# One plain gate moved into the first stage of a transformer layer, and w_out's operands moved later

## The chip, the core and the metric

The kernel runs on one core of a Trainium2 chip. The metric is device time in microseconds (us) for one execution. TensorE (PE in the profile) does the matmuls, ScalarE (ACT) and VectorE (DVE) make the operands and empty the accumulators, GpSimd (POOL) helps in the attention stage, and SyncE (SP) issues every DMA in one queue, in order.

## The reference, cut to what matters

One layer on a sequence of 1024 tokens with 1024 channels, float32:

```python
h = x @ w_in                                   # 8 blocks of q/k/v columns, then 2 x 1024 gate columns
qa, ka, va, qb, kb, vb, ga, gb = split(h)
y_a = chunk_band_attention(qa, ka, va) @ w_proj_a      # 8 heads, softmax over a band, learned bias
y_b = stick_breaking_attention(qb, kb, vb) @ w_proj_b  # 8 heads, running products, strictly causal
mix = (sigmoid(ga + bias) * y_a + sigmoid(gb + bias) * y_b) @ w_out
x = layer_norm(ALPHA * x + mix)
x = layer_norm(ALPHA * x + (silu(x @ w_g) * (x @ w_u)) @ w_ffn_out)
```

The 2048 gate columns are 16 gates of 128 columns each. Gate `i` is the product of a 1024 x 128 granule of `w_in` with all of `x`, and its value is needed only when the two attention branches are merged.

## The kernel before, in words

**Precision.** Every operand is split into a high and a low part (`split`, lines 110 to 112: a cast on ACT, then a subtraction on DVE), and each product is three matmuls: high x high, high x low, low x high. A block of 128 rows by 512 columns is one matmul instruction.

**Two ways to make a product.** A *plain* product of a 1024 x 128 granule with `x` is 8 x 3 matmuls for each half of the tokens, 48 in all. A *pair* of granules can instead be made by a 2 x 2 block scheme with 7 products (steps `p1`, `p2`, `p6`, `p5`, `p7`, `p3`, `p4` in `pair_steps`, 12 matmuls each, 84 instead of 96), which needs sums of the blocks of `x` (`s13`, `s24`, made once on DVE) and sums of the blocks of the two granules (`prep_right`, `prep_last`, made per pair on DVE and ACT).

**Stages.** The order of time is:

1. The q/k pairs. The first one (`project_plain(0)`) is made plainly, 96 matmuls into four accumulators of the `tr` and `pv` banks, because `s13` and `s24` are not there yet; its function returns a closure `take` that empties the accumulators. Then `run_pairs(1, N_QK, 2, also)` makes pairs 1 to 7 by the 7 products, with steps `p1` and `p2` of pairs 1 and 2 ahead of all others, since these two need only the left granule and parts of `x`, no sums.
2. `v_stage`, the values of both branches.
3. `run_pairs(N_QK, ...)`: five gate pairs (work items 8 to 12), which make gates 0 to 9 and store them to DRAM (`g_dr`).
4. The attention stage: 8 heads of branch A, then 8 of branch B. Its PE work consists of scores (`sc_a`, `sc_b`), transposes of the weights (`tp_a`, `tp_b`) and products with the values (`pv_a`, `pv_b`). Between them stands *fill*: single matmuls from a generator, `fill_all`, which makes the six plain gates 10 to 15 (288 matmuls) and then the projection of branch A (192). `FILL` says how many fill matmuls a head of A and of B draws; 8 x (18 + 42) = 480 is the sum of both.
5. The projection of branch B, `w_out`, the first LayerNorm, the FFN and the second LayerNorm.

**w_out's operands.** `w_out` is also multiplied by the 7-product scheme. Its 28 operand tiles are made early and stored to DRAM (`wo_dr`) by `wo_right(part)`, 12 parts (four blocks of three parts: the first loads two raw tiles and makes two operands, the second makes three, the third two). The table `wo_at` says behind which step `(i, j)` of the pairs each part stands, `i` the work item and `j` the index of the step in the list `p1, p2, p6, p5, p7, p3, p4`.

**Buffers.** Tiles take turns in groups of slots of 4 KB per partition. The ones that matter here: `gt` (3 slots: raw granules, gate results), `op` (8: split granules), `kp` (4), `v` (2: raw `w_out` tiles, later the heads' values), and `qs`, `kh`, `kl` (2 each), which are dealt out in turn by `cycle(QK, ...)` to the pairs' results and to w_out's operands, and later by name to the heads' q and k. `xt` (16) holds the split `x`. Accumulators are eight banks: `mm` 2, `sc` 2, `tr` 3, `pv` 1.

**What sets the order.** The program is traced in the order of the code; a scheduler then orders each engine's instructions by that priority and by a cost model, so an instruction whose inputs and slots are ready in the model can stand earlier than in the code. On the chip each engine takes its instructions strictly in the order so fixed, and an instruction that must wait holds up all behind it on its engine, SP's DMA issues too.

Lines that the change and the prediction touch: `FILL` (42), `split` (111, 112), `prep_left`, `prep_right`, `prep_last` (133 to 168), the products of the pairs (178), `project_plain` (118 to 121, 324, 325), `wo_right` (494 to 515), `load_gate` and `load_w` (524 to 526), `gate` (542, 545), `soft_block` and `stick_block` (632 to 670), the transposes and their split (696, 111, 112), the products with the values (710, 711, 720).

Of the kernel before, what the change touches and what calls it, by code (L numbers as in the profile page):

```python
# [38 lines left out]
PACKS = ((((4,), (5, 7), (3,), (2, 0), (6, 1)), ((7,), (6, 4), (5,))),  # L39
         (((4,), (5,), (6,), (7,), (3,), (2, 0), (1,)), ((7,), (6, 4), (5,))))  # L40

FILL = (18.0, 42.0)

# [5 lines left out]
def hybrid_trunk_kernel(ctx: ExitStack, tc, x, xt, w_in, w_v, b_gate, rel_bias, w_proj,  # L51
# [14 lines left out]
    def slot(tag, name, dtype=F32):  # L66
        return pool.tile([P, 1024], dtype, tag=tag, name=name, bufs=SLOTS[tag])
# [3 lines left out]
    def cycle(tags, name, dtype=F32):  # L71

        turn_of[tags] = turn_of.get(tags, -1) + 1
        return slot(tags[turn_of[tags] % len(tags)], name, dtype)

    QKV = ("qs", "kh", "kl", "v")
    QK = QKV[:3]

    def bank(tag, name):
        return ps.tile([P, HW], F32, tag=tag, name=name, bufs=BANKS[tag])  # L80
# [6 lines left out]
    dma = nc.sync.dma_start  # L87
# [22 lines left out]
    def split(dst_h, dst_l, src):  # L110
        nc.scalar.copy(dst_h, src)  # L111
        nc.vector.tensor_tensor(dst_l, src, dst_h.bitcast(F32), ALU.subtract)  # L112

    def mm3(acc, pairs):
        n = len(pairs)
        i = 0
        for lh, ll, rh, rl in pairs:
            mm(acc, lh, rh, start=(i == 0), stop=False)
            mm(acc, lh, rl, start=False, stop=False)
            i += 1  # L120
            mm(acc, ll, rh, start=False, stop=(i == n))
# [13 lines left out]
    def prep_left(W, nm, src, tag="op"):  # L135
        L = W["L"] = slot("gt", f"wL{nm}")
        load_then(L, src)
        W["hl"] = split_w(L, f"wl{nm}", tag)

    def split_w(raw, nm, tag):  # L140
        h = slot(tag, f"{nm}h", F32R)
        l = slot(tag, f"{nm}l", F32R)
        split(h, l, raw)
        return h, l
# [15 lines left out]
    def prep_last(W, nm, tag):  # L160

        c = slot(tag, f"wc{nm}", F32R)
        split(c[:, LO], c[:, HI], W["R"][:, HI])
        W["c"] = c
# [69 lines left out]
    N_GATE = 5  # L234
# [3 lines left out]
    def left(i):  # L238
        prep_left(Wa[i], f"p{i}", w_in[work[i][2]])

    def right(i):
        prep_right(Wa[i], f"p{i}", w_in[work[i][3]], "op")
        prep_last(Wa[i], f"p{i}", "kp")

    sops = {}
    s_tags = iter(["bw"] * 9 + ["pt"] * 4 + ["yt"] * 3)
    for kt in range(4):
# [21 lines left out]
        dma(xraw[k][:, HI], xt[k * P:(k + 1) * P, HI])  # L269
    for k in order_k:  # L270
        split(xh[k][:, HI], xl[k][:, HI], xraw[k][:, HI])
    for kt in range(4):
        a, b = xraw[kt], xraw[kt + 4]
        s13 = slot("kp", f"s13_{kt}")
        s24 = slot("kp", f"s24_{kt}")
        nc.vector.tensor_tensor(s13[:, LO], a[:, HI], b[:, HI], ALU.add)
        nc.vector.tensor_tensor(s24[:, LO], s13[:, LO], a[:, LO], ALU.subtract)
        nc.vector.tensor_tensor(s24[:, HI], b[:, LO], s24[:, LO], ALU.subtract)
        nc.vector.tensor_tensor(s13[:, HI], a[:, LO], a[:, HI], ALU.subtract)
        for src, nm in ((s24, "s24"), (s13, "s13")):  # L280
            split(*sops[nm, kt], src)
# [19 lines left out]
    def store_hl(d, hi, lo):  # L301
        for h in range(2):
            rows = slice(h * DH, (h + 1) * DH)
            dma(d[h * P:h * P + DH], hi[rows].bitcast(F32))
            dma(d[h * P + DH:(h + 1) * P], lo[rows])

    def project_plain(i):

        W, pair = Wa[i], work[i][1]
        accs = {}  # L310
        for half in (LO, HI):
            for side, key in enumerate(("hl", "hr")):
                tag = "pv" if side and half == HI else "tr"
                acc = accs[side, half.start] = bank(tag, f"plain{side}_{half.start}")
                wh, wl = W[key]
                mm3(acc, [(wh[:, k * P:(k + 1) * P], wl[:, k * P:(k + 1) * P],
                           xh[k][:, half], xl[k][:, half]) for k in (0, 4, 1, 5, 2, 6, 3, 7)])
        def take():
            for side, (scale, d) in enumerate(((-0.125, q_dr), (1.0, k_dr))):
                h = cycle(QK, f"hi{side}_{i}", F32R)  # L320
                t = cycle(QK, f"lo{side}_{i}")
                for half in (LO, HI):
                    acc = accs[side, half.start]
                    nc.scalar.activation(h[:, half], acc, AF.Copy, scale=scale)
                    nc.vector.scalar_tensor_tensor(t[:, half], acc, scale,
                                                   h[:, half].bitcast(F32),
                                                   ALU.mult, ALU.subtract)
                store_hl(d[pair], h, t)
        return take
# [36 lines left out]
    def run_pairs(lo, hi, first, also):  # L366

        steps = {i: project(i) for i in range(lo, hi)}
        for i in range(lo, lo + first):
            steps[i][0]()  # L370
            steps[i][1]()
        for i in range(lo, hi):
            for j, p in enumerate(steps[i][2:] if i < lo + first else steps[i]):
                p()
                if j == 0 and i + 1 < hi:
                    right(i + 1)
                if j == 1 and lo + 2 <= i + 2 < hi and i + 2 >= lo + first:
                    left(i + 2)
                also(i, j)
# [138 lines left out]
    def load_w(srcs, name, raw, hl, lo_eng):  # L518
        r = raw(f"wr_{name}")
        hi = hl(f"wh_{name}", F32R)  # L520
        lo = hl(f"wl_{name}", F32R)
        srcs = srcs if isinstance(srcs, list) else [(slice(0, 1024), srcs)]
        for cs, src in srcs:
            dma(r[:, cs], src)
        nc.scalar.copy(hi, r)
        lo_eng.tensor_tensor(lo, r, hi.bitcast(F32), ALU.subtract)
        return hi, lo

    def of(tag):
        return lambda name, dtype=F32: slot(tag, name, dtype)  # L530

    def load_gate(i, lo_eng):
        return load_w(w_in[24 + (i % 2) * 8 + i // 2], f"g{i}", of("op"), of("op"), lo_eng)

    def gate(i, w):
        gt = slot("gt", f"gate{i}")
        for hf, cs in enumerate((LO, HI)):
            acc = bank("mm", f"gps{i}_{hf}")
            for k in range(KT):
                ks = slice(k * P, (k + 1) * P)  # L540
                for j, (lw, rx) in enumerate(((w[0], xh), (w[0], xl), (w[1], xh))):
                    mm(acc, lw[:, ks], rx[k][:, cs], start=(k == j == 0),  # L542
                       stop=(k == KT - 1 and j == 2))
                    yield 1.0
            nc.scalar.copy(gt[:, cs], acc)
        dma(g_dr[i], gt)

    left(2)
    take = project_plain(0)
    right(1)  # L550
    take()
    wo_at = {(2, 4): 0, (3, 6): 1, (4, 6): 2, (5, 6): 3, (6, 2): 4, (6, 6): 5,
             (8, 6): 6, (9, 2): 7, (9, 6): 8, (10, 6): 9, (11, 2): 10, (11, 6): 11}

    def also(i, j):
        if (i, j) == (2, 2):
# [7 lines left out]
    run_pairs(1, N_QK, 2, also)  # L564
    v_stage()
    run_pairs(N_QK, len(work), 0, also)
    first_gate = 2 * N_GATE
    first_w = load_gate(first_gate, nc.vector)


# [161 lines left out]
    def fill_all():  # L732
        w = first_w
        for i in range(first_gate, 16):
            nxt = load_gate(i + 1, nc.gpsimd) if i < 15 else load_proj(0, 0, "op", nc.gpsimd)
            for n, unit in enumerate(gate(i, w)):
                if i == 15:
                    if n in (6, 12, 18, 26):
                        load_y((6, 12, 18, 26).index(n))
                    if n in (28, 34, 40, 46):  # L740
                        split_y((28, 34, 40, 46).index(n), nc.gpsimd)
                yield unit
            w = nxt
# [54 lines left out]
    def fill_until(t):  # L798
        while state["t"] < t and not state["done"]:
            try:  # L800
                state["t"] += next(fill)
            except StopIteration:
                state["done"] = True
# [35 lines left out]
    for hd, hidx, g, st, pos, box in vsteps:  # L839
# [12 lines left out]
        last = goal  # L852
        goal += FILL[hd["br"]] / nhead
        fill_until(0.5 * (last + goal))
# [30 lines left out]
    def load_pair(n):  # L885
        return load_w([(cs, w_proj[WO[n] + 4 * j][:, HW:2 * HW]) for j, cs in enumerate((LO, HI))],
                      f"yB{n}", of("op"), of("op"), nc.vector)

    for n in range(4):
        w = load_pair(n)  # L890
# [194 lines left out]
    def take(tt, half, bank_, first):  # L1085
        dst = acc_t[tt][:, half]
        if first:
            nc.vector.scalar_tensor_tensor(dst, dst, ALPHA, bank_, ALU.mult, ALU.add)
        else:
            nc.vector.tensor_tensor(dst, bank_, dst, ALU.add)  # L1090
# [254 lines left out]
```

## Time and profile before

| | us |
|---|---|
| median of 3 runs | 1443.78 (1442.98 to 1445.72) |
| the profiled execution, whole | 1447.72 |
| the profiled execution, span of the page | 1445.9 |
| PE busy | 1402.8 (97%) |
| DVE, ACT, POOL busy | 1023.3, 685.9, 312.3 |
| plain pair, first to last matmul | 6.08 to 31.84 |
| pairs 1 to 7 and the values | 32.06 to 251.99 |
| gate pairs | 252.2 to 347.4 |
| attention | 347.4 to 669 |

The views of the profile are told where they are used. Times in them are microseconds from the start of the span. A row of the timeline gives start, duration, engine, line of the kernel, operation, output and inputs by name, shapes, how many like ones were merged, and in brackets how long the engine was idle before it and for whom it waited. A matmul of 512 columns is shown with a duration of 0.39 us, but the next one starts 0.227 us after it: they overlap, and the distance between starts is what counts. A row of the view of stretches gives the length of a stretch, then busy time and number of instructions of PE, of its weight loads (PEld), of DVE, ACT and POOL, then the granted PE clock, the share of DMA time and GB/s.

### The profile page before, as it was taken

The numbers are of one execution on the slowest core, as the hardware profiler recorded it, in microseconds if no ns is written. First come the engines' busy times: TensorE is split into PE (matmuls) and PEld (weight loads), VectorE is DVE, ScalarE is ACT, GpSimd is POOL, SyncE is SP. The second block draws the span as 40 slices with busy tenths as digits, with TensorE's granted clock in tenths as the row PEclk, the third lists the DMA queues.
The fourth block names the chain that finished last, engine by engine and source line by source line (L and its number), as shares of the span: only waits on it lengthen the run. The fifth ranks groups of instructions, "written<-read, shape, count | busy, mean of one in ns | idle before, by whom it ended". The sixth has DMA issues, their size and how long they took to land.

```text
span 1445.9 us, 18799 instructions
## 1 busy us (share of the span) xinstructions
PE 1402.8 (97%) x6592; PEld 1157.1 (80%) x6592; DVE 1023.3 (71%) x1587; ACT 685.9 (47%) x1196; POOL 312.3 (22%) x339
## 2 busy tenths in 40 slices
PE   8999999999999998999999999999999999999997
PEld 6777788887888787788887778888888788888886
DVE  7866658753878887887869995555565544885896
ACT  6444344444877778784323543333333332444540
POOL 0000000003434768662304121111111011300012
PEclk9999999999999999999999999999999999999999
DMA  6577837759656466657861243233222226853521
GB/s 233 160 208 237 268 103 275 263 207 258 188 163 184 137 188 195 214 176 268 328 234 73 80 138 113 99 110 109 96 88 94 94 102 243 327 187 111 173 82 73
DMA packets 98574, 248.75 MB, mean 172 GB/s; under 512 B 10400, under 2 KB 26784, under 8 KB 98480
## 3 DMA queue, kind: packets, MB, share of 16 engines
q1 hardware_dynamic: 98480, 247.56, 51.9%
q8 instruction: 52, 0.85, 0.2%
q14 instruction: 42, 0.34, 0.1%
HBM read 164.39 MB, written 83.13 MB: 171 GB/s over the span
## 4 chain that ended last, share of the span: by engine, by line
PE 82%; DVE 8%; ACT 3%; issue 3%; DMA 2%; POOL 1%; SPq 0%; POOLq 0%; DVEq 0%; ACTq 0%
PE dn L1238 14%; PE sxf L178 14%; PE sxp L178 8%; PE szf L178 6%; PE v L418 5%; PE ops L1097 5%; PE szp L178 4%; PE gps L542 4%; PE syf L178 3%; PE yAps L758 2%; PE syp L178 2%; PE tp_b L696 2%; PE tp_a L696 1%; PE sc_a L599 1%; DMA xraw<-in_xt_dram 1%
## 5 line engine op out<-in xcount | busy, mean ns | idle before, releaser
L1238 PE MATMUL dn<-dr,dl 128*128 128x512 f32 x924 | 209.7, 389 | 0.0
L1238 PEld LDWEIGHTS dn<-dr,dl 128*128 128x128 f32 x924 | 173.4, 188 | 36.2 <-DVE x L1090 0.3
L667 DVE TENSOR_TENSOR_SCAN kp_b<-kp_b,ident_ps 128x512 f32<-128x512 f32 (+3 forms) x96 | 93.1, 971 | 25.9 <-ACT kp_b L665 22.2
L670 POOL TENSOR_TENSOR w_b<-w_b,kp_b 128x511 f32<-128x511 f32 (+3 forms) x96 | 100.6, 1057 | 50.2 <-DVE kp_b L667 44.0
L111 ACT CAST dl<-raw 128x512 fp32r<-128x512 f32 x77 | 47.2, 622 | 83.5 <-PE dn L1238 61.9
L1097 PE MATMUL ops<-wr,wl 128*128 128x512 f32 x336 | 78.8, 392 | 0.0
L934 POOL TENSOR_TENSOR mv<-mv,neghalf 128x1 f32<-128x1 f32 x16 | 25.7, 1608 | 237.3 <-DVE mv L933 237.3
L619 POOL MEMSET bias<- 64x64 f32 x8 | 1.2, 145 | 335.0 <-ACT bias L618 335.0
L1097 PEld LDWEIGHTS ops<-wr,wl 128*128 128x128 f32 x336 | 62.5, 188 | 12.5
L112 DVE TENSOR_TENSOR dl<-raw,dl 128x512 fp32r<-128x512 f32 x77 | 53.5, 701 | 26.1 <-ACT dl L111 25.9
L665 ACT ACTIVATE kp_b<-sc_b 128x512 f32<-128x512 f32 (+3 forms) x96 | 49.6, 516 | 23.2 <-PE sc_b L600 20.4
L640 POOL TENSOR_SCALAR w_a<-w_a,st_a 128x640 f32<-128x640 f32 (+2 forms) x64 | 44.6, 704 | 62.3 <-DVE st_a L639 47.6
L178 PE MATMUL szf<-x1S63h,wcf 128*128 128x512 f32 x168 | 55.2, 390 | 1.2 <-ACT gt L208 1.2
L1035 POOL TENSOR_TENSOR sb<-h 128x512 f32<-128x512 f32 x10 | 15.8, 1582 | 187.9 <-PE syf L178 136.9
L112 DVE TENSOR_TENSOR pt_b<-tp_b,pt_b 128x512 fp32r<-128x512 f32 (+1 forms) x80 | 48.4, 621 | 9.0 <-ACT pt_b L111 8.7
L191 DVE TENSOR_TENSOR gt<-sxf,gt 128x512 f32<-128x512 f32 x21 | 14.4, 687 | 54.5 <-PE sxf L178 54.5
L696 PE MATMUL tp_b<-ident,w_b 128*128 128x128 f32 x288 | 45.0, 274 | 5.0 <-DVE pt_b L112 5.0
L666 ACT ACTIVATE w_b<-sc_b 128x511 f32<-128x511 f32 (+3 forms) x96 | 49.7, 518 | 0.0
L111 ACT CAST pt_b<-tp_b 128x512 fp32r<-128x512 f32 (+1 forms) x80 | 45.3, 574 | 8.6 <-PE tp_b L696 8.2
L637 ACT ACTIVATE w_a<-w_a,st_a 128x640 f32<-128x640 f32 (+2 forms) x64 | 44.4, 695 | 10.5 <-DVE st_a L632 9.9
L1036 POOL TENSOR_TENSOR sa<-h,h 128x512 f32<-128x512 f32 x10 | 15.9, 1588 | 147.6 <-PE sxf L178 120.6
L153 DVE TENSOR_TENSOR taf<-wRf,wLf 128x512 f32<-128x512 f32 x21 | 15.6, 742 | 43.1 <-DMA wRf<-in_w_ffn_in_dram 43.1
(1512 smaller groups left out, 4209.7 us busy)
## 6 DMA issues: line engine op xcount, KB each, us to landing
raw<-left_dr SPq DMA_DIRECT2D x77, 256.0 KB, 3.0
wo_dr<-wo SPq DMA_DIRECT2D x28, 512.0 KB, 4.2
wr<-wo_dr SPq DMA_DIRECT2D x28, 512.0 KB, 7.9
wLf<-in_w_ffn_in_dram SPq DMA_DIRECT2D x22, 512.0 KB, 4.8
wRf<-in_w_ffn_in_dram SPq DMA_DIRECT2D x22, 512.0 KB, 4.3
rows<-in_w_ffn_out_dram SPq DMA_DIRECT2D x22, 512.0 KB, 6.3
left_dr<-h SPq DMA_DIRECT2D x33, 256.0 KB, 2.0
v_dr<-vst SPq DMA_DIRECT2D x16, 512.0 KB, 4.0
```

The source lines that it names most:

```text
L111: nc.scalar.copy(dst_h, src)
L112: nc.vector.tensor_tensor(dst_l, src, dst_h.bitcast(F32), ALU.subtract)
L178: mm(acc, lw[:, ks], rx, start=(first and kt == i == 0), stop=(kt == 3 and i == 2), skip_group_check=not first)
L418: mm(banks[mt], xs[lw][:, ms], o[:, rx], start=(fresh and kt == n == 0), stop=(kt == 3 and n == 2), skip_group_check=not fresh)
L542: mm(acc, lw[:, ks], rx[k][:, cs], start=(k == j == 0), stop=(k == KT - 1 and j == 2))
L665: nc.scalar.activation(kp[:, c0:e], sc[:, 0:n], AF.Sigmoid, scale=-1.0)
L666: nc.scalar.activation(be[:, m0:e], sc[:, m0 - c0:n], AF.Sigmoid)
L667: nc.vector.tensor_tensor_scan(kp[:, c0:e], kp[:, c0:e], ident_ps()[:, 0:n], kp[:, c0 - 1:c0] if c0 else 0.0, ALU.mult, ALU.bypass if c0 e ...
L670: nc.gpsimd.tensor_tensor(be[:, m0:e], be[:, m0:e], kp[:, m0 - 1:e - 1], ALU.mult)
L696: tr(tp[:, j:j + P], wt[qb - q0][:, (kb - qb) * P:(kb - qb + 1) * P], ident)
L1097: mm(acc, lw, rx, start=(fresh and n == m == 0), stop=(n == 3 and m == 2), skip_group_check=not fresh)
L1238: mm(acc, lw, rx, start=(fresh and steps[s][1] == n == 0), stop=(last and n == 2), skip_group_check=not fresh)
```

## The change: what it does

- Gate 10, the first of the six plain gates, leaves the fill of the attention stage. Its granule is loaded behind the right half of `x` into a `gt` slot and split (ACT and DVE) ahead of the sums `s13` and `s24`. Its 48 matmuls stand behind the plain pair and ahead of the first products of pairs 1 and 2; its two accumulators (`mm`) are emptied by ACT into a `cycle(QK)` slot, and it is stored to `g_dr`.
- `left(2)`, the load and split of pair 2's left granule, now stands behind `project_plain(0)` instead of ahead of it.
- `FILL` goes from (18, 42) to (16, 38); the fill is five plain gates (240 matmuls) and the projection (192), 8 x (16 + 38) = 432.
- `wo_at`: parts 0, 1, 2 stand in q/k pairs 4, 5 and 6 (before, parts 0 to 5 stood in pairs 2 to 6), and parts 3 to 11 in the gate pairs 8 to 12 (before, parts 6 to 11 in pairs 8 to 11).

```diff
-FILL = (18.0, 42.0)
+FILL = (16.0, 38.0)
...
+    def gate_src(i):
+        return w_in[24 + (i % 2) * 8 + i // 2]
...
     for k in order_k:
         split(xh[k][:, HI], xl[k][:, HI], xraw[k][:, HI])
+    first_gate = 2 * N_GATE
+    G0 = slot("gt", "wG0")
+    dma(G0, gate_src(first_gate))
+    gate_w = split_w(G0, "wg0", "op")
     for kt in range(4):
         a, b = xraw[kt], xraw[kt + 4]
...
-    def gate(i, w):
-        gt = slot("gt", f"gate{i}")
+    def gate(i, w, gt=None):
+        gt = gt or slot("gt", f"gate{i}")
...
+    take = project_plain(0)
     left(2)
-    take = project_plain(0)
     right(1)
     take()
-    wo_at = {(2, 4): 0, (3, 6): 1, (4, 6): 2, (5, 6): 3, (6, 2): 4, (6, 6): 5,
-             (8, 6): 6, (9, 2): 7, (9, 6): 8, (10, 6): 9, (11, 2): 10, (11, 6): 11}
+    for _ in gate(first_gate, gate_w, cycle(QK, "gate0")):
+        pass
+    first_gate += 1
+    wo_at = {(4, 6): 0, (5, 6): 1, (6, 6): 2, (8, 2): 3, (8, 6): 4, (9, 2): 5, (9, 6): 6,
+             (10, 2): 7, (10, 6): 8, (11, 2): 9, (11, 6): 10, (12, 2): 11}
...
     run_pairs(N_QK, len(work), 0, also)
-    first_gate = 2 * N_GATE
     first_w = load_gate(first_gate, nc.vector)
```

More of the change, by code (lines that the diff above doesn't have):

```diff
@@ L532, in load_gate @@
     def load_gate(i, lo_eng):
-        return load_w(w_in[24 + (i % 2) * 8 + i // 2], f"g{i}", of("op"), of("op"), lo_eng)
-    def gate(i, w):
-        gt = slot("gt", f"gate{i}")
+        return load_w(gate_src(i), f"g{i}", of("op"), of("op"), lo_eng)
+    def gate(i, w, gt=None):
+        gt = gt or slot("gt", f"gate{i}")
         for hf, cs in enumerate((LO, HI)):
```

## The prediction

> **What bounds the kernel now.** I read the page first, then the view of stretches around the places that the diff touches, then what PE waited for there, then single rows. The page's busy shares and the chain that ended last:
>
> ```profile
> PE 1402.8 (97%) x6592; PEld 1157.1 (80%) x6592; DVE 1023.3 (71%) x1587; ACT 685.9 (47%) x1196; POOL 312.3 (22%) x339
> ...
> PE 82%; DVE 8%; ACT 3%; issue 3%; DMA 2%; POOL 1%; SPq 0%; POOLq 0%; DVEq 0%; ACTq 0%
> ```
>
> PE is the bound over the whole, and the change takes no matmul away: 48 are moved. So it can win only the time in which PE stands still, and where that is must be seen stage by stage. The first stage, by stretches:
>
> ```profile
> 20.00:30.00 10.00, 10.00 (x45) 8.28 (x45) 10.00 (x16) 6.82 (x10) 0.00 (x0) 1.00 0.26 76
> 30.00:40.00 10.00, 9.56 (x42) 7.61 (x41) 10.00 (x13) 5.08 (x6) 0.00 (x0) 1.00 0.57 156
> 40.00:50.00 10.00, 7.87 (x32) 5.57 (x32) 10.00 (x14) 4.69 (x7) 0.00 (x0) 1.00 0.58 182
> ```
>
> From 20 to 50 us DVE (the third pair of numbers) is busy all the time, while PE falls from 45 matmuls in 10 us to 42 and 32. DVE sets the pace there, and PE has the hole. The waits of PE from 30 to 205 us name it:
>
> ```profile
> PE szp L178 <- ACT wap4h L111: 1.6, 1, 1.6
> PE sxp L178 <- ACT c L195: 1.6, 2, 1.4
> PE sxp L178 <- ACT c L204: 1.4, 2, 0.7
> PE sxp L178 <- ACT wlp7h L111: 1.1, 1, 1.1
> PE sxp L178 <- DVE c L191: 0.5, 1, 0.5
> PE szp L178 <- DVE wap4l L112: 0.5, 1, 0.5
> PE sxp L178 <- DVE wlp2l L112: 0.4, 1, 0.4
> ```
>
> Its size comes from starts of matmuls, since a shown duration of 0.39 us hides part of a gap:
>
> ```profile
> 32.06 0.39 PE L178 MATMUL sxp<-xh,wlp1h 128*128 128x512 f32 x1
> ...
> 37.28 0.39 PE L178 MATMUL syp<-xh,wlp1l 128*128 128x512 f32 x1
> ...
> 45.26 0.50 PE L178 MATMUL sxp<-s24h,wbp1h 128*128 128x512 f32 x1 [1.42 <-ACT c L195]
> ...
> 49.26 0.50 PE L178 MATMUL sxp<-s13h,wap1h 128*128 128x512 f32 x1 [0.68 <-ACT c L204]
> ...
> 57.56 0.39 PE L178 MATMUL sxp<-xh,wbp1h 128*128 128x512 f32 x1
> ```
>
> The first two rows stand 23 matmuls apart: 5.22 / 23 = 0.227 us for one, back to back. Between the first row and the last lie 8 products of 12, so 96 x 0.227 = 21.8 us of work in 25.5 us: the hole is 3.7 us.
>
> **The change, part by part.** *The gate in the first stage.* 48 x 0.227 = +10.9 us of PE work behind the plain pair. In its shade DVE goes on with what the products after the hole wait for:
>
> ```profile
> 37.74 1.22 DVE L112 TENSOR_TENSOR wlp2l<-wLp,wlp2h 128x1024 fp32r<-128x1024 f32 x1
> ...
> 44.76 1.22 DVE L112 TENSOR_TENSOR wbp1l<-tbp,wbp1h 128x1024 fp32r<-128x1024 f32 x1
> ...
> 46.49 1.22 DVE L112 TENSOR_TENSOR wap1l<-tap,wap1h 128x1024 fp32r<-128x1024 f32 x1
> ```
>
> The gate's low part adds one such subtraction (1.22 us) to the full DVE, so wbp1l is ready at 46.0 + 1.2 = 47.2 and wap1l at 48.9. PE, with the gate ahead, asks for wbp1l at 32.06 + 96 x 0.227 = 53.9. Slack 6.7 us, so the hole closes: -3.7 us. Bounds: 0 (the gate's matmuls themselves wait, and p1 and p2 of two pairs queue behind them on PE) to -3.7. I take the end, as the need comes 6.7 us after the supply. Other queues: ACT gets a cast and two copies, and is 68% busy or less; SP gets a load of 512 KB ahead of pair 2's left and pair 1's right granule, and a store behind the last copy. DVE comes to those granules only at 37.7 us (first row) and later, so a load that lands a few us later costs nothing; without that cover it would be one load, 4 to 6 us.
>
> *w_out's first parts leave pairs 2 and 3.* At 98 to 101 us PE waits for pair 4's right operands, and the queue of SP shows where they lost time:
>
> ```profile
> 81.51 1.98 SPq L494 DMA_DIRECT2D wo_dr<-wo  x2
> 83.94 0.81 SPq L133 DMA_DIRECT2D wRp<-in_w_in_dram  x1
> ```
>
> ```profile
> 98.13 0.39 PE L178 MATMUL sxp<-xh,wbp3l 128*128 128x512 f32 x1
> 100.14 0.50 PE L178 MATMUL szp<-s13h,wap4h 128*128 128x512 f32 x1 [1.62 <-ACT wap4h L111]
> 100.48 0.40 PE L178 MATMUL szp<-s13l,wap4h 128*128 128x512 f32 x1
> 101.40 0.50 PE L178 MATMUL szp<-s13h,wap4l 128*128 128x512 f32 x1 [0.53 <-DVE wap4l L112]
> ```
>
> Starts 2.01 and 0.92 us apart instead of 0.227: 2.5 us lost. The granule's load was issued 2.4 us later for two w_out stores, and these no longer exist there (the first part now stands in pair 4). I take -2.5, bounds 0 and -2.5. The other waits of the list (wlp7h 1.1, half of L204 0.7, L191 0.5: 2.3 us) lie in pairs 6 and 7, where w_out keeps one part each; I leave them. Scaled like the two places measured by starts ((3.7 + 2.5) against 4.8 in the list) they are 3.0 us, the bound for more gain.
>
> *w_out in the gate pairs: nine parts instead of six.* A part is up to four DVE operations of 0.69 us and three casts on ACT, three stores, and two loads in every third part. The gate pairs have room:
>
> ```profile
> 260.00:280.00 20.00, 20.00 (x90) 16.57 (x89) 13.66 (x19) 8.08 (x12) 0.00 (x0) 1.00 0.74 265
> ```
>
> PE is full and DVE at 68% although two parts lie in this stretch. Cost 0 here. The last part moves from behind step p4 of pair 11 to behind p6 of pair 12, 3 x 12 x 0.227 = 8.2 us later, toward the heads' loads:
>
> ```profile
> 318.20 1.67 SPq L494 DMA_DIRECT2D wo_dr<-wo  x2
> ...
> 333.77 1.08 SPq L583 DMA_DIRECT2D kl<-k_dr  x2
> ```
>
> Stores at 318.2 + 1.7 + 8.2 = 328, landed (4.2 us by the issues below) at 332: before kl was loaded anyway. I take 0; the other end is a last part that runs no earlier than its place in the code, 347.4 - 48 x 0.227 = 336.5, some 3 us for its operands, 4.2 for the store and 6.4 for the load of kl: 350, a wait of 3 us before the first scores at 347.4.
>
> ```profile
> wo_dr<-wo SPq DMA_DIRECT2D x28, 512.0 KB, 4.2
> ...
> kl<-k_dr SPq DMA_DIRECT2D x32, 256.0 KB, 6.4
> ```
>
> *The attention stage loses the 48 matmuls* (2 of 18 in a head of A, 4 of 42 in one of B): 8 x 2 x 0.227 + 8 x 4 x 0.227 = -10.9 us, if PE sets the pace there. Four heads' lengths (the transposes of a head end at the right border):
>
> ```profile
> 413.60:429.20 15.60, 15.47 (x98) 13.43 (x97) 12.77 (x42) 12.09 (x29) 5.59 (x11) 1.00 0.58 170
> 461.70:480.80 19.10, 17.10 (x100) 13.78 (x99) 16.69 (x32) 15.95 (x37) 12.38 (x23) 1.00 0.41 110
> 526.20:548.60 22.40, 22.40 (x130) 19.32 (x128) 18.40 (x25) 16.09 (x38) 12.59 (x20) 1.00 0.71 236
> 572.80:601.30 28.50, 23.02 (x128) 19.04 (x127) 20.77 (x27) 21.75 (x45) 20.80 (x26) 1.00 0.73 240
> ```
>
> The first and third are heads as most are: PE full, DVE 82%, and 0.45 or 0.91 us less would leave DVE at 84 or 86%. But does the chain scores, softmax, transposes keep up when less fill lies between? The tightest link is the last weight tile of a head's first turn:
>
> ```profile
> 412.44 1.59 POOL L640 TENSOR_SCALAR w_a<-w_a,st_a 128x640 f32<-128x640 f32 x2 [1.60 <-DVE st_a L639]
> ```
>
> ```profile
> 415.00 0.60 PE L696 MATMUL tp_a<-ident,w_a 128*128 128x128 f32 x4
> ```
>
> ```profile
> 522.06 3.06 POOL L670 TENSOR_TENSOR w_b<-w_b,kp_b 128x448 f32<-128x448 f32 x3 [0.38 <-DVE kp_b L667]
> ```
>
> ```profile
> 527.92 0.60 PE L696 MATMUL tp_b<-ident,w_b 128*128 128x128 f32 x4
> ```
>
> The margin is 415.00 - 414.03 = 1.0 us in A and 527.92 - 525.12 = 2.8 us in B. By `LEAD` those tiles are begun three steps ahead of the turn; three steps lose 3 x 2/8 x 0.227 = 0.2 us of fill in A and 3 x 4/10 x 0.227 = 0.3 in B. The margins hold. The second and fourth head are those with waits. Five heads are such (the first, sixth and last of A, the fourth and fifth of B), and together they lose 3 x 2 + 2 x 4 = 14 fill matmuls, 3.2 us. Fill ahead of a wait for ACT or DVE saves nothing when it goes; I let half of it be lost: -10.9 + 1.6 = -9.3. Bounds: -10.9, and 0 if all heads turn out bound elsewhere. The gate takes work of other engines along (a cast and two copies of ACT, a subtraction of POOL), which I count as nothing.
>
> ```profile
> L526 POOL TENSOR_TENSOR wl_g<-wr_g,wh_g 128x1024 fp32r<-128x1024 f32 x5 | 12.0, 2403 | 13.6 <-ACT wh_g L525 12.0 <-issue 1.3 <-PE gps L542 0.3
> ```
>
> *Sum:* +10.9 - 3.7 - 2.5 + 0 - 9.3 = -4.6 us. The profiled execution took 1447.72 us around its span of 1445.9, 3.9 above the median; the terms are differences, so I set them against the median: 1443.8 - 4.6 = **1439.2 us**.
>
> The Trainium skill (Perfetto Trace Analysis, section Identifying the Most-Contended Engine) says that a kernel with several regimes can gain by interleaving them; read that way, fill belongs beside the attention's DVE and ACT work, and taking some away speaks against this change. By that rule the heads would give nothing back, and the sum would be +4.7; that is the first rival below. The row of the third head, PE 22.40 of 22.40, speaks against it.
>
> **The rivals.** *Fill was cover* (slower). The heads have no PE time to give back: with less fill each waits at its first turn or for its accumulators. Price: +10.9 - 3.7 - 2.5 = +4.7, **1448.5 us**. For it: five heads with waits of 1.3 to 6 us, and a margin of only 1.0 us in A. Against: full PE in the others. It decides once less than 1.8 of the 10.9 us come back.
>
> *w_out comes too late for the heads* (no change): both parts of a pair share six slots with the pair's results, and SP stands still before a store whose operand is not ready. A wait of 3 us before the first scores: 1439.2 + 3 = **1442.2 us**. Against it: 14 us between kl's load and its first use.
>
> *The hole stays* (no change; the change doesn't do what it says): the scheduler puts the first products ahead of the gate, or DVE falls further behind. +3.7: **1442.9 us**. Against it: 6.7 us of slack.
>
> *All waits go* (faster still): the other 3.0 us of the q/k pairs and the 1.6 us in the heads: **1434.6 us**. For it: pairs 5 and 6 hold one w_out part each where pair 6 held two, and ACT and POOL lose a gate's work in the heads.
>
> **How the numbers follow.** A difference under 0.2% (2.9 us) can hardly be told from none here. Chances: forecast 0.45, fill was cover 0.13, w_out late 0.13, hole stays 0.12, all waits go 0.17. Faster is the forecast and the last, less 0.02 for a forecast that comes out at its weak edge: 0.60; same 0.27; slower 0.13. The range runs from the last rival, 1434.5, to 1446, which takes in both rivals of no change and half return from the heads (+5.4, 1443.0) with a wait on top, and leaves out the full price of the slow one.
>
> **What would show it.** Right: the gate's matmuls between 32 and 43 us, p6 of pair 1 near 54 without a wait; no wait for pair 4's right operands; first scores at 347.4 + 10.9 - 6.2 = 352 without idle PE; heads of 15.1 and 21.5 us. Wrong: waits of PE before those scores, heads of A still at 15.6 or of B at 22.4, or new waits in pairs 5 to 7.

## The result, and the profile after

The changed kernel took **1433.87 us** (median of 6 runs, 1432.86 to 1438.62) against 1444.15 us of the kernel before beside it (6 runs, 1442.98 to 1446.06): a ratio of **0.9933, 95% interval [0.9917, 0.9949]**, so faster by 0.5 to 0.8%. Run once more, later and beside other runs of the kernel before, it gave 0.9917 [0.9901, 0.9934]. The forecast was 1439.2; the direction is right, the gain is more than twice the size forecast, and the time lies just below the range.

The page of the changed kernel, its busy shares:

```profile
PE 1401.2 (98%) x6592; PEld 1157.2 (81%) x6592; DVE 1021.5 (71%) x1588; ACT 686.0 (48%) x1196; POOL 309.4 (22%) x338
```

PE has as many instructions as before; the span fell from 1445.9 to 1432.0 us at the same PE work. So what went is time in which PE stood still, and the views say where. The first stage, in the view of stretches:

```profile
30.00:40.00 10.00, 10.00 (x46) 8.29 (x45) 10.00 (x14) 5.23 (x7) 0.00 (x0) 1.00 0.53 141
40.00:50.00 10.00, 10.00 (x45) 8.05 (x45) 9.96 (x14) 4.51 (x7) 0.00 (x0) 1.00 0.58 190
```

Where 42 and 32 matmuls were in 10 us there are now 46 and 45, and DVE is as full as it was: the same DVE work now lies under PE's. What PE does there, and when DVE delivers, in rows of the timeline:

```profile
31.22 0.39 PE L121 MATMUL plain<-xh,wrp0l 128*128 128x512 f32 x1
31.45 0.39 PE L549 MATMUL gps<-xh,wg0h 128*128 128x512 f32 x1
...
42.10 0.39 PE L549 MATMUL gps<-xh,wg0l 128*128 128x512 f32 x1
...
53.37 0.39 PE L178 MATMUL sxp<-s24h,wbp1h 128*128 128x512 f32 x1
```

```profile
45.23 1.23 DVE L112 TENSOR_TENSOR wbp1l<-tbp,wbp1h 128x1024 fp32r<-128x1024 f32 x1
```

The gate runs from 31.45 to 42.3, one matmul behind the other, and step p6 of pair 1 starts at 53.37 with no bracket, so with no wait. The low part of its weights has been ready since 46.46, 6.9 us earlier (forecast: 6.7 us of slack). PE's waits from 20 to 340 us, the whole rest of the q/k pairs, the values and nearly all gate pairs, are an empty list; this is the full answer:

```profile
core 0 of [0], span 1432.0 us
engine line waited for: us in total, times, longest us
```

The first scores and the first matmul of the projection of branch B bound the attention stage:

```profile
347.95 0.30 PE L608 MATMUL sc_a<-kh,qs 128*128 128x320 f32 x1
...
657.06 0.40 PE L118 MATMUL yBps<-yh,wh_yB 128*128 128x512 f32 x1
```

The first scores stand at 347.95 instead of 347.4: 48 more matmuls (10.9 us) cost the first stage 0.5 us. The attention takes 309.1 us instead of 321.6. Three of its heads, cut at the same borders as before:

```profile
414.10:429.50 15.40, 15.30 (x97) 12.90 (x96) 12.62 (x41) 12.18 (x30) 5.66 (x11) 1.00 0.55 172
520.70:542.30 21.60, 21.60 (x125) 18.60 (x124) 17.79 (x24) 19.67 (x42) 16.77 (x20) 1.00 0.70 206
566.30:590.40 24.10, 22.08 (x126) 18.42 (x124) 22.22 (x28) 19.18 (x42) 17.20 (x25) 1.00 0.61 187
```

The first two are usual heads: 15.4 and 21.6 us where they took 15.6 and 22.4. The last, the fifth head of B, is the surprise: 24.1 instead of 28.5 us, with 22.08 us of PE work in it instead of 23.02. Less fill alone would make that 0.9 us; 3.5 us of idle PE went too.

### The profile page after: what moved, and what is told of

It reads as the page before. It is cut to its first block, busy times and chain, and to the rows that moved or that the text cites. A ratio compares the mean times of both kernels' runs of the same rounds, so it can differ in the third digit from the quotient of the medians.

```text
span 1432.0 us, 18804 instructions
## 1 busy us (share of the span) xinstructions
PE 1401.2 (98%) x6592; PEld 1157.2 (81%) x6592; DVE 1021.5 (71%) x1588; ACT 686.0 (48%) x1196; POOL 309.4 (22%) x338
## 4 chain that ended last, share of the span: by engine, by line
PE 84%; DVE 7%; ACT 3%; DMA 3%; issue 2%; POOL 0%; POOLq 0%; DVEq 0%; SPq 0%; ACTq 0%
PE sxf L178 15%; PE dn L1247 15%; PE sxp L178 9%; PE szf L178 7%; PE v L425 5%; PE ops L1106 5%; PE szp L178 5%; PE syf L178 4%; PE gps L549 3%; PE syp L178 2%; PE tp_b L705 2%; PE yAps L767 1%; DVE kp_b L676 1%; PE tp_a L705 1%; PE yBps L118 1%
## 5 line engine op out<-in xcount | busy, mean ns | idle before, releaser
L112 DVE TENSOR_TENSOR pt_a<-tp_a,pt_a 128x512 fp32r<-128x512 f32 x64 | 41.6, 652 | 6.9 <-ACT pt_a L111 6.4
```

## The experiments

All ratios below are to the kernel before, run on the same chip. "First scores" and "attention" are read as in the rows above, from one profiled execution of each kernel. In some of these executions PE's granted clock falls to 0.50 for 3.4 us or more behind a wait (the last section has them all); where a length that is used holds such a stretch, the text says so.

**The kernel before, once more.** Needed because the profiled execution of before was 3.9 us above its median.

> The kernel before once more, for a second profile of it: the first profiled execution took 1447.72 us, 3.6 above the median of its runs. Whatever the theory, the ratio is 1.000. If the waits in the q/k stage (10 us after the start) and in the fourth and fifth head of B (8 us) belong to the kernel, they stand again with the same size; if part of them belonged to that execution, the excess of 3.6 us is missing there.

Ratio 1.0002 [0.9992, 1.0011]. First scores at 346.8, attention 321.4 us, and from there to the end of the span 774.7 us, as in the changed kernel (774.9), where the first profile of before had 776.9. Of the 3.0 us between the two spans 2.2 lay behind the attention and had nothing to do with the change; the two stages that matter repeat within 0.6 us.

**The gate alone.** Edit to the changed kernel:

```diff
-    wo_at = {(4, 6): 0, (5, 6): 1, (6, 6): 2, (8, 2): 3, (8, 6): 4, (9, 2): 5, (9, 6): 6,
-             (10, 2): 7, (10, 6): 8, (11, 2): 9, (11, 6): 10, (12, 2): 11}
+    wo_at = {(2, 4): 0, (3, 6): 1, (4, 6): 2, (5, 6): 3, (6, 2): 4, (6, 6): 5,
+             (8, 6): 6, (9, 2): 7, (9, 6): 8, (10, 6): 9, (11, 2): 10, (11, 6): 11}
```

> The change with w_out's parts left where they stood before (parts 0 to 5 in pairs 2 to 6). The changed kernel lost none of the 10 us of waits of PE that the kernel before had in the q/k stage; two theories say which edit took them. Theory W (w_out's stores held up the loads): the gate closes the hole behind the plain pair alone, and the waits of pairs 4, 6 and 7 (5.5 us by the starts of matmuls) stay; first scores near 353.5 us, and the whole 4 to 6 us faster than before, near 1439. Theory L (lead): the gate gives DVE, ACT and SP some 6.7 us of lead on PE, which lasts to the end of the stage and covers those waits wherever w_out stands; first scores near 348 to 349, the whole 9 to 10 us faster, near 1434.5.

Measured: 1439.06 us, ratio 0.9949 [0.9936, 0.9963]. PE's waits from 20 to 340 us in this kernel:

```profile
PE szp L178 <- ACT c L208: 0.8, 1, 0.8
PE sxp L178 <- ACT c L204: 0.7, 1, 0.7
PE sxp L178 <- DVE c L191: 0.6, 1, 0.6
```

The hole is gone, as it should be. So is the wait for pair 4's right operands (wap4h 1.6, wap4l 0.5), though the w_out stores still stand ahead of its load. So neither theory holds as written: the lead covers pair 4's wait, and the others stay with w_out's parts. What is left lies at 150 to 183 us, in pairs 6 and 7: PE waits for ACT to empty accumulators, and ACT for this, in its own list of waits from 140 to 185 us:

```profile
ACT c L195 <- DMA q_dr<-hi: 3.6, 2, 2.5
...
ACT c L208 <- DMA k_dr<-c: 2.3, 1, 2.3
```

ACT can't write a pair's result because its slot still holds an older one whose store hasn't landed. SP is held up by w_out in the meantime, at five stores, but these are not what delays the store. They end at 158.11, and the pair's next stores leave from 161.36 on, the first as soon as ACT has made its operand (160.28 + 1.05 = 161.33):

```profile
148.83 9.28 SPq L501 DMA_DIRECT2D wo_dr<-wo  x5
...
161.36 0.45 SPq L311 DMA_DIRECT2D k_dr<-hi  x1
```

```profile
160.28 1.05 ACT L354 ACTIVATE hi<-c 128x1024 fp32r<-128x1024 f32 x1
```

What w_out's parts share with the pairs besides SP is the turn of the slots and ACT's queue; which of the two makes these waits was not isolated.

The first scores come at 350.9, 2.9 us behind the changed kernel's (2.4 behind those of its second profile below).

**w_out's places alone.** The reverse edit: the kernel before with the new `wo_at`.

> The kernel before with w_out's parts at the changed places, and nothing else of the change. Theory W: the waits of pairs 4, 6 and 7 go, 5.5 us, the hole of 3.7 us stays; first scores near 342, the whole near 1438.5. Theory L: without the gate's lead DVE stays just ahead of PE; only the wait at pair 4 whose load stood behind the stores can go, 0 to 2.5 us; the whole 1441.5 to 1444.

Measured: 1437.44 us, ratio 0.9944 [0.9931, 0.9956]; first scores at 341.0, 5.8 us ahead of the kernel before, run again. PE's waits from 20 to 340 us:

```profile
PE sxp L178 <- ACT c L195: 1.4, 1, 1.4
PE sxp L178 <- ACT c L204: 0.7, 1, 0.7
PE sxp L178 <- DVE wlp2l L112: 0.4, 1, 0.4
PE sxp L178 <- DVE c L191: 0.3, 1, 0.3
```

The hole behind the plain pair stays (the first three rows), pair 4's wait goes, and so do the waits of pairs 6 and 7 but for 0.3 us, as theory W has it. The load of pair 4's right granule stands where the forecast wanted it, at 80.97 us with no w_out store ahead, 2.6 us earlier than in the kernel before, run again:

```profile
80.97 0.81 SPq L133 DMA_DIRECT2D wRp<-in_w_in_dram  x1
```

The attention is 319.7 us, 1.7 less than in the kernel before, run again. The two edits alone give 0.51 and 0.56%, 1.07 together, and the whole change 0.67 to 0.83: they overlap, since either removes pair 4's wait.

**Three w_out parts left in the early pairs.** The kernel before, with parts 0 to 2 where they were and only parts 3 to 11 moved:

```diff
-    wo_at = {(2, 4): 0, (3, 6): 1, (4, 6): 2, (5, 6): 3, (6, 2): 4, (6, 6): 5,
-             (8, 6): 6, (9, 2): 7, (9, 6): 8, (10, 6): 9, (11, 2): 10, (11, 6): 11}
+    wo_at = {(2, 4): 0, (3, 6): 1, (4, 6): 2, (8, 2): 3, (8, 6): 4, (9, 2): 5, (9, 6): 6,
+             (10, 2): 7, (10, 6): 8, (11, 2): 9, (11, 6): 10, (12, 2): 11}
```

> The kernel before, with w_out's first three parts in pairs 2, 3 and 4 as they were and none in pairs 5 and 6 (parts 3 to 11 in the gate pairs). It tells whose waits belong to which parts. If the wait at pair 4 comes from the stores of the parts in pairs 2 and 3, it stands with its 2.5 us; if the waits in pairs 6 and 7 (3.2 us) come from the three parts in pairs 5 and 6 that share slots and SP's queue with the pairs' results, they are gone; the hole of 3.2 us behind the plain pair stays. First scores then at 346.8 - 3.2 = 343.6 us, the whole 3 to 5 us faster than before. If DVE's load as such makes the waits, all of them shrink alike.

Measured: 1439.46 us, ratio 0.9962 [0.9948, 0.9977]. PE's waits from 20 to 345 us:

```profile
PE szp L178 <- ACT wap4h L111: 1.6, 1, 1.6
PE sxp L178 <- ACT c L195: 1.4, 1, 1.4
PE sxp L178 <- ACT c L204: 0.7, 1, 0.7
PE szp L178 <- DVE wap4l L112: 0.5, 1, 0.5
PE sxp L178 <- DVE wlp2l L112: 0.4, 1, 0.4
```

Pair 4's wait is back, nothing is left in pairs 6 and 7. The first scores stand at 344.3, with 3.4 us at clock 0.50 behind pair 4's wait. With the two kernels before it, this ties the waits to their makers: pair 4's to the parts in pairs 2 and 3, those of pairs 6 and 7 to the three parts in pairs 5 and 6.

**The gate and the three early parts.** The changed kernel with that same table.

> The changed kernel, with w_out's first three parts at pairs 2, 3 and 4 (where the kernel before has them) instead of 4, 5 and 6; the other nine stay in the gate pairs. What it tells apart: whether the wait of 2.5 us for pair 4's right operands is closed by the gate's lead alone. Theory L (the gate delays PE by 11 us against DVE, ACT and SP, and pair 4's operands are made in that lead): no wait at pair 4, first scores at 348 us, time as the changed kernel. Theory W (the wait is the w_out stores' and stays where they stay): 2.5 us of waits at pair 4, first scores at 350.5, time 2.5 us above the changed kernel.

Measured: 1433.59 us, ratio 0.9914 [0.9899, 0.9929], not to be told from the changed kernel (0.9917 beside it). PE's list of waits from 20 to 340 us is empty here too, and the first scores stand at 347.9. So pair 4's wait is closed by the gate's lead alone. Of w_out's move, what the changed kernel needs is that parts 3 to 5 leave pairs 5 and 6; the move of parts 0 to 2 brings nothing beside the gate.

**Gate 10 left out.** The kernel before without gate 10's 48 matmuls, and with the new `FILL`:

```diff
-FILL = (18.0, 42.0)
+FILL = (16.0, 38.0)
...
         dma(g_dr[i], gt)
+        if i == 11:
+            dma(g_dr[10], gt)
...
-    first_gate = 2 * N_GATE
+    first_gate = 2 * N_GATE + 1
```

> The kernel before with gate 10 left out altogether (its place in DRAM gets gate 11's values, so that the output is not the reference's), FILL (16, 38). It prices what the attention stage gives back for 48 matmuls. If PE sets the pace in the heads: 10.9 us, and some more where a wait goes with the gate's ACT and POOL work (the changed kernel's attention stage was 12.5 us shorter in the profiled executions); the whole near 1432 to 1433. If fill was cover: less than 5 us, 1439 or above.

Measured: 1433.74 us, ratio 0.9919 [0.9905, 0.9932]. The first scores stay at 346.7, and the attention takes 311.1 us, 10.3 less than in the kernel before, run again. But its profile holds a stretch at lower clock, in the fifth head of B (third number from the end):

```profile
580.00:585.00 5.00, 5.00 (x20) 4.09 (x19) 4.19 (x6) 1.17 (x2) 2.87 (x6) 0.66 1.04 234
```

That is up to 5 x 0.34 = 1.7 us, an estimate, which the kernel before does not have. The ratio, taken over all runs, says 11.7 us (9.8 to 13.7). So the heads gave back 10.3 to 12 us for 48 matmuls of 10.9 us: about all. The gate alone agrees: it is 7.4 us faster by its ratio although its first scores come 3.5 to 4.1 us later than before, so some 11 us came from what follows. In this kernel PE waits 0.3 us for `yv_b` in the heads of B; in the two profiles of the kernel before it is 3.7 and 2.9, all in the fifth.

**Who holds the fifth head of B.** In the kernel before, run again, PE's and ACT's rows there:

```profile
575.00 0.50 PE L710 MATMUL pv_b<-pt_b,v 128*128 128x512 f32 x1 [1.12 <-ACT yv_b L720]
583.93 0.50 PE L710 MATMUL pv_b<-pt_b,v 128*128 128x512 f32 x1 [1.73 <-ACT yv_b L720]
```

```profile
571.95 1.05 ACT L525 CAST wh_y<-wr_y 128x1024 fp32r<-128x1024 f32 x1 [1.88 <-DMA wr_y<-in_w_proj_dram]
...
574.34 0.61 ACT L720 COPY yv_b<-pv_b 128x512 f32<-128x512 f32 x1
...
581.86 1.04 ACT L525 CAST wh_y<-wr_y 128x1024 fp32r<-128x1024 f32 x1 [2.51 <-POOL yl L788]
...
583.29 0.59 ACT L720 COPY yv_b<-pv_b 128x512 f32<-128x512 f32 x1
```

ACT stands in the cast of the projection's weights (1.88 us for their load, 2.51 for a subtraction of POOL), and the copy that frees the accumulator for PE stands behind it. The load for the second cast left late itself: SP issues it just after POOL's subtraction of the weights before has ended (574.10 + 2.38 = 576.48):

```profile
574.10 2.38 POOL L526 TENSOR_TENSOR wl_y<-wr_y,wh_y 128x1024 fp32r<-128x1024 f32 x1
```

```profile
576.50 0.81 SPq L524 DMA_DIRECT2D wr_y<-in_w_proj_dram  x2
```

The edit gives that copy to DVE in three heads of B:

```diff
-                    nc.scalar.copy(both[:, gs], pv[0])
+                    if hd["br"] == 1 and hd["n"] in (3, 4, 5):
+                        nc.vector.tensor_copy(both[:, gs], pv[0])
+                    else:
+                        nc.scalar.copy(both[:, gs], pv[0])
```

> The kernel before, with one edit: in the fourth to sixth head of B DVE empties the accumulator of the products with the values (yv_b) instead of ACT. What it tells apart: why PE waits some 3 us for yv_b in the fifth head of B before, and not with fewer fill matmuls. Theory C (ACT takes its instructions in order and stands in the cast wh_y of the projection's weights, behind their load and a subtraction of POOL): the wait of PE for yv_b there goes, head five is some 3 us shorter than 27.7, and the time is 0 to 3 us below the kernel before, as DVE has six more copies of about 0.7 us. Rival D (PE is late there for some other reason that the row only names, DVE or POOL): the head stays at 27 to 28.5 us, with the wait under another name; time as before.

Measured: 1446.06 us, ratio 1.0000 [0.9991, 1.0010]. The numbers are rival D's (the head takes 28.3 us, with the wait under another name, time as before), the rows are theory C's. The wait for `yv_b` fell from 2.9 to 0.4 us, and 3.2 us came in its place, in a PE and an ACT row:

```profile
582.00 0.50 PE L599 MATMUL sc_b<-kh,qs 128*128 128x512 f32 x1 [3.23 <-ACT w_b L666]
```

```profile
580.55 1.04 ACT L525 CAST wh_y<-wr_y 128x1024 fp32r<-128x1024 f32 x1 [4.14 <-DMA wr_y<-in_w_proj_dram]
```

ACT still stands in that cast, 4.14 us for the load, and PE now waits for the next of ACT's products that stand behind it, a `w_b` that frees an accumulator of the scores. So the copy was only the first in the queue; what costs the 3 us is ACT held in that cast, by a late load or by POOL. In the changed kernel ACT's waits for `wr_y` in the attention are 0.2 us in all, and this wait of PE is not there. The Trainium skill (PSUM — Partial Sum Buffer, section Engine vs sequencer instructions) calls ScalarE's queue strictly first in, first out; the rows at 571.95 and 574.34 agree with that, and so do 580.55 and the wait at 582.00.

**The fill otherwise dealt.** The changed kernel with the 432 fill matmuls divided otherwise between A and B:

```diff
-FILL = (16.0, 38.0)
+FILL = (12.0, 42.0)
```

> The changed kernel with the fill taken from the heads of A alone, FILL (12, 42). In B the projection of branch A then starts in the same head as in the kernel before ((240 - 96) / 42 = 3.4 heads in; 2.9 in the changed kernel). Theory P (place): the waits of 2.9 to 3.7 us for the emptied accumulator in the fifth head of B, where ACT stood in a cast that waited for the load of the projection's weights, come with that place: they return here, and the whole is 2 to 4 us slower than the changed kernel. Theory N (number): fewer fill matmuls in a head of B make room on ACT and POOL; then those waits return as well, and heads of B are 22.4 us long. Both agree on B; the heads of A decide if A is bound by PE: 15.3 - 4 x 0.227 = 14.4 us each if it is, no shorter than 15.1 if the softmax chain ends there.

Measured: 1436.25 us, ratio 0.9941 [0.9926, 0.9955]; the attention is 312.2 us, 3.1 more than in the changed kernel. The 32 matmuls moved (7.3 us) made A 5.6 us shorter, 111.0 instead of 116.5 (its usual heads some 14.7), so A can do with less; but B grew by 8.7, from 192.6 to 201.3. The old wait returned in its fifth head, as both theories said, and behind it the clock is at 0.50 for 6.8 us, up to 3.4 us lost by estimate. The wait, in PE's list from 347 to 672 us:

```profile
PE pv_b L719 <- ACT yv_b L729: 3.1, 1, 3.1
```

ACT stands in the cast again, here 4.4 us for POOL's `yl` and not for the load.

The other way, `FILL = (20.0, 34.0)`:

> The changed kernel with more fill in A and less in B, FILL (20, 34); the projection starts (240 - 160) / 34 = 2.4 heads into B. If PE sets the pace in all undisturbed heads: 16.2 us in A and 20.7 in B, and the whole within 2 us of the changed kernel, the difference being waits. If 34 is too little cover for the chain in B: heads of B stay at 21.3 or more, and the whole is 4 us slower or worse. Theory P: no wait for the emptied accumulator behind the load of the projection's weights; theory N: none either.

Measured: 1440.56 us, ratio 0.9968 [0.9957, 0.9979], attention 315.6 us. A grew by 8.6 us (up to 1.7 of it at clock 0.50) and B lost 2.1, where 7.3 were moved. B's quiet heads went down to 20.5 us, but the waits took most of that back:

```profile
PE tp_b L705 <- DVE pt_b L112: 6.0, 7, 2.0
PE sc_b L608 <- ACT w_b L675: 4.0, 4, 2.1
PE sc_a L608 <- DVE st_a L641: 3.6, 3, 2.1
```

In the changed kernel the same rows are 3.2, 2.2 and 0.4 us. With 34 fill matmuls in a head of B, part of the fill is cover.

**A second gate in the first stage.** Gate 11 follows gate 10, its granule in a `v` slot, and `FILL` goes on to (14, 34):

```diff
+    G1 = slot("v", "wG1")
+    dma(G1, gate_src(first_gate + 1))
+    gate_w1 = split_w(G1, "wg1", "op")
     for _ in gate(first_gate, gate_w, cycle(QK, "gate0")):
         pass
     first_gate += 1
+    for _ in gate(first_gate, gate_w1, cycle(QK, "gate1")):
+        pass
+    first_gate += 1
```

> The changed kernel with a second plain gate behind the first in the first stage, FILL (14, 34). There is no wait left for it to fill, so the first stage grows by all 10.9 us. The attention stage gives back 10.9 us if it is bound by PE, and one to two more if a gate's work on ACT and POOL counts there: the whole between 2 us faster and 1 us slower than the changed kernel. If with 34 in a head of B the chain becomes the bound, it is 3 to 8 us slower.

Measured: 1439.51 us, ratio 0.9965 [0.9952, 0.9978], so 4.6 to 6.9 us slower than the changed kernel by that one's two ratios. The first scores move to 359.1, the full 11.1 us: there was no idle PE left to fill. The attention falls to 305.7, by 3.4 us and not by 10.9 (A stays at 116.5, with up to 1.7 us at clock 0.50 in it, B goes from 192.6 to 189.2); by the ratios it gives back 4.2 to 6.5. PE's waits from 347 to 672 us say why:

```profile
PE tp_b L711 <- DVE pt_b L112: 6.5, 8, 2.0
PE sc_b L614 <- ACT w_b L681: 2.8, 3, 2.1
PE sc_a L614 <- DVE st_a L647: 2.0, 1, 2.0
```

The rival "fill was cover" is true of about half of the next 48 matmuls, and was not of these. It may not be the count alone: A gave back 5.6 us at 12, and at 14 nothing that can be told from the 1.2 us by which A differs between the two profiles of the changed kernel and the 1.7 of the clock. Which loads and casts meet a head may matter as well; the runs don't separate the two.

**The changed kernel once more.**

> The changed kernel once more, unedited. What it tells: how far its time and the waits of single heads repeat. Expected: within 0.2% of the changed kernel's 1433.9 us, ratio 0.993 to the kernel before, first scores at 348.0, attention 309 us, waits of PE in the heads within 3 us of the first profile's, at the same places (the fifth head of A or B not among those with a wait for yv_b). If the attention is 311 us, as with the gate left out, the 2 us between the two were the execution's own and not the change's.

Measured: 1433.23 us, ratio 0.9917 [0.9901, 0.9934], first scores at 348.5, attention 308.6 us, waits of PE 10.7 us in the list of the stage (11.0 in the first profile). So the attention is 12.3 to 12.8 us shorter than in the kernel before, run again. The 2 us beyond the kernel without gate 10 are not the change's: that profile has the stretch at clock 0.66, and these two have none in the attention. By the ratios the two kernels are alike (0.9919; 0.9933 and 0.9917), though the changed one has 0.5 to 1.7 us more in the first stage.

W_out's new places alone took 1.7 us from the attention, with no such stretch in either profile. By PE's waits these are in the first heads of A; the kernel before, run again (347 to 400 us):

```profile
PE tp_a L696 <- POOL w_a L640: 1.1, 2, 0.9
PE sc_a L599 <- DVE st_a L632: 0.7, 2, 0.5
```

and the kernel with w_out's new places alone (341 to 394 us):

```profile
PE sc_a L599 <- DVE st_a L632: 0.2, 1, 0.2
```

Which link between w_out's table and the first heads does it was not isolated.

## Why the prediction was right in direction and wrong in size

The forecast was a sum. Each term of it against what the runs showed:

| term | forecast | measured | from |
|---|---|---|---|
| gate's 48 matmuls in the first stage | +10.9 | +10.9 | rows 31.45 to 42.10, 0.227 us apart |
| hole behind the plain pair | -3.7 | all of it gone | empty list; kept in both kernels with w_out alone moved |
| wait at pair 4 | -2.5 | all of it gone | empty list |
| other waits, pairs 6 and 7 | 0 | -2.4 to -2.9 | first scores, the gate alone against the whole change |
| attention, 48 fill matmuls fewer | -9.3 | -10.3 to -12 | gate 10 left out, profile and clock |
| attention, w_out's new places | 0 | -1.7 | w_out's places alone |
| attention, both together | -9.3 | -12.3 to -12.8 | the changed kernel's two profiles |
| sum, the attention by its last row | -4.6 | -10.0 to -11.0 | -10.3 by the medians |

The first four rows make +1.8 to +2.3 us of the first stage; from profile to profile its end moved by 0.5 to 1.7 us. How the attention's gain divides between the fill and w_out is not settled; that it is 3.0 to 3.5 us larger than forecast is.

- **The hole** closed for the reason given, DVE's lead under the gate's matmuls, with 6.9 us of slack where 6.7 were worked out. The rival "the hole stays" is out.
- **Pair 4's wait** went, and the load moved as forecast (w_out alone). But it was put down to the w_out stores alone; the gate's lead closes it as well (gate alone, and gate with the three early parts). The size was right; the cause named was one of two, each sufficient.
- **"The other waits of the list lie in pairs 6 and 7, where w_out keeps one part each; I leave them."** This step failed, with nearly half of the miss (2.4 to 2.9 us put at nothing). That one part each would stay was taken as no change, but three parts had been there: with those three the waits stand (w_out as before, the gate alone), with one part in pair 5 and one in pair 6 none of them is left in the changed kernel. The text had the right bound (3.0 us) and gave it to a rival.
- **"I let half of it be lost: -10.9 + 1.6 = -9.3."** Mis-sized, and the other half of the miss: the heads gave back 10.3 to 12 us, so about all, and 12.3 to 12.8 together with w_out's move. The heads with waits did lose fill, but the wait of the fifth head of B, the largest, was ACT standing in a cast ahead of the copy. It was gone with 38 fill matmuls in a head of B and back with 42; whether by their number or by where the projection starts, the runs don't tell.
- **w_out in the gate pairs, "Cost 0 here", and the start of the attention, "I take 0".** Not a cost, as forecast: the gate pairs have no wait, and the rival "w_out comes too late for the heads" is out. But its bounds named no gain, and w_out's places alone gain 1.7 us; beside the gate that gain can't be told from the fill's.
- **The rivals.** "All waits go" (1434.6, chance 0.17) came true in the first stage. In the heads the gain is as large as it says and larger (12.3 to 12.8 against 10.9), and yet not all waits went: PE still waits 10.7 to 11.0 us there. "Fill was cover" was wrong here and in part right one gate further, where 48 matmuls bring back 3.4 to 6.5 us. The Trainium skill (Perfetto Trace Analysis, section Optimization Strategy, and not the section that the prediction names) says that interleaving regimes may help. Here both directions were measured, and the row of the stage (PE 22.40 of 22.40 in a head of B) spoke rightly for this step. It would not have for the next: in the changed kernel that row is as full (21.60 of 21.60).
- **What would show it:** the gate between 32 and 43, p6 of pair 1 near 54, no wait at pair 4, a head of 21.5 in B: met (31.45 to 42.3, 53.37, none, 21.6). The head of A came out at 15.4, between the 15.1 of the forecast and the 15.6 that it named as a sign of being wrong. First scores at 352: missed by 4, the waits of pairs 6 and 7 and 1 us that the rows don't divide further.

**Still open:** why ACT is held in the cast of the projection's weights with 42 fill matmuls in a head of B and not with 38, and the links from w_out's table to pairs 6 and 7 and to the first heads of A.

## What to carry to other kernels

When work is moved to fill a hole, list every wait of the stage, and ask of each whether the edit also moves something out of its way: the waits of pairs 6 and 7 hung on parts that the same edit moved, and belonged in the sum. Filler can be moved out of a stage only as far as the stage gives the time back, and a full engine in the usual cycle does not tell how far that is: here the first 48 matmuls came back almost whole, the next 48 by a third to 60%, with PE full in the usual head of B before either step. So the step has to be measured at each size. A wait that names a copy may be owed to another instruction ahead of it on that engine; moving the copy elsewhere then only renames the wait.

## What the runs showed that was not expected

In seven of the thirteen profiled executions PE ran at half pace for a few microseconds behind a wait. The kernel with three w_out parts left early did so after pair 4's wait. Its rows, and the stretch around them (clock in the third column from the end):

```profile
99.67 0.50 PE L178 MATMUL szp<-s13h,wap4h 128*128 128x512 f32 x1 [1.62 <-ACT wap4h L111]
...
100.93 0.79 PE L178 MATMUL szp<-s13h,wap4l 128*128 128x512 f32 x1 [0.52 <-DVE wap4l L112]
101.52 0.63 PE L178 MATMUL szp<-s13h,wap4h 128*128 128x512 f32 x1
101.95 0.63 PE L178 MATMUL szp<-s13l,wap4h 128*128 128x512 f32 x1
```

```profile
100.00:105.00 5.00, 4.48 (x14) 3.23 (x12) 5.00 (x7) 3.03 (x5) 0.00 (x0) 0.66 0.93 292
```

The same stretch of the kernel before, run again, with the same two waits (1.62 and 0.53):

```profile
100.00:105.00 5.00, 4.47 (x20) 3.51 (x20) 5.00 (x7) 2.87 (x5) 0.00 (x0) 1.00 0.95 294
```

Starts are 0.43 us apart instead of 0.227, the granted clock is 0.66 in the stretch instead of 1.00, and 14 matmuls are done instead of 20. Read in steps of half a microsecond, the clock is 0.50 for 3.4 us. All such stretches, but for the last 10 us of the spans:

| kernel | PE's wait before it, us, and its end | clock 0.50 |
|---|---|---|
| three parts left early | 1.62, 99.67 | 100.6 to 104.0 |
| the gate alone | 1.73, 550.12 | 551.2 to 554.6 |
| the gate alone | 1.82, 584.96 | 585.3 to 588.7 |
| gate 10 left out | 1.83, 579.64 | 581.1 to 584.5 |
| FILL (12, 42) | 3.10, 575.69 | 574.6 to 581.4 |
| FILL (20, 34) | 2.06, 396.10 | 396.4 to 399.8 |
| a second gate | 2.01, 416.54 | 417.9 to 421.3 |
| the gate and the three early parts | 1.82, 577.17 | 577.4 to 580.8 |

Each lasts 3.4 us, or twice that, and begins during the wait or within 1.5 us of its end. Other waits as long left the clock at 1.00: 2.17 us in the kernel before, 2.49 in the changed kernel once more, 3.23 with `yv_b` on DVE. So in some executions a wait of about 2 us costs up to 1.7 us more than itself (half of 3.4, an estimate), as much as some of the differences that single profiles are read for here. The Trainium skill (TensorE: Matmul & The Clock Gate, Part 1) has the clock halved after about 3.4 us without work, judged in windows that run on by themselves, with 426.7 ns from start to start while it is halved. The 0.43 us and the length of 3.4 us agree. That a whole idle window is needed does not agree: none of these waits is that long, and the first was 1.62 us. What decides which wait is followed by such a stretch, no run here shows.
